# 32 bytes more per tile: operand and weight tiles of a float32 split-product kernel at other places in SBUF

## The chip, the cores and the metric

The kernel runs on one core of a Trainium2 chip. The metric is device time in microseconds (us). Two timed runs of the kernel before gave 1836.11 and 1837.32 us, a median of 1836.71 us. Durations of single instructions come from one further execution that the hardware profiler recorded.

## The reference

Two transformer-like blocks on 512 tokens of width 1024, all in float32. Nearly all of the work is matrix products of the activations with weight matrices; what lies between them is elementwise.

```
hn = rms_norm(h, g_mix_pre);  proj = hn @ w_in                 # 1024 -> 8192
br_a = spatial_gating(gelu(z_sgu)) @ w_sgu_out
br_b = conformer_conv(z_conv)      @ w_conv_out                # depthwise, 31 taps
br_c = multiscale_pool(z_pool)     @ w_pool_out
h = h + rms_norm((gates . (br_a, br_b, br_c)) @ w_out)
h = h + rms_norm((silu(f_gate) * f_up) @ w_ffn_out)            # 1024 -> 2 x 2816 -> 1024
h = h + sigmoid(h @ w_ple_gate) * (p @ w_ple)
# second block
proj = rmsnorm(x) @ w_in_2
oa = gated_delta_rule(conv(q, k, v))                           # a scan over chunks of 64 tokens, 4 heads
ob = chunk_band_attention(q, k, v)                             # 8 heads
x = x + (sig(ga) * (oa @ w_branch_a) + sig(gb) * (ob @ w_branch_b)) @ w_out_2
x = x + (silu(gate) * up) @ w_down                             # 1024 -> 2 x 2816 -> 1024
out = rmsnorm(x)
```

## The kernel before, in words

Activations lie feature-major in SBUF: a product with 1024 input features reads eight tiles of 128 partitions x 512 tokens. To keep float32 accuracy with the one-pass `float32r` matmul, each operand is split in a high and a low half, and each 128x128 piece of a product is three matmuls (`mm3`, lines 153 to 156): high weights by high operand (L154), high weights by low operand (L155), low weights by high operand (L156). The stationary side is a 128-column slice of a weight tile, the moving side is an operand tile of 512 tokens, or of 256 where `linear_halves` does the tokens in two halves. `linear_tm` (L325 to L327) has the sides changed: the operand is stationary and the weights move.

The tiles in question:

- `raw`: a weight chunk as it lands by DMA, 128 x 1024 float32, two buffers (`prep`).
- `whi`, `wlo`: its high and low half, four buffers each. ScalarE writes `whi` (L99), VectorE writes `wlo` as `raw - whi` (L102).
- `xh`, `xl` and `th`, `tl`: two sets of operand tiles, high and low half, eight buffers of 128 x 512 each (`pair`). Operands beyond eight tiles (the products over 2816 features) and a few others are `fh`, `fl`, which come from other pools by the same helper `blk`.

All of them come from pools that hand out buffers of a tag in turn. `emit` runs the steps in order and prepares weight chunks two steps ahead of the step that uses them, so that TensorE goes from one product to the next.

Where the tiles start, as the built program places them, in bytes within 256, buffer by buffer:

| tile | before | after the change |
|---|---|---|
| `whi` (4 buffers) | 32, 32, 32, 32 | 32, 64, 96, 128 |
| `wlo` (4 buffers) | 32, 32, 32, 32 | 160, 192, 224, 0 |
| `xh`, `th` (8 buffers each) | 32 in all | 0, 32, 64, 96, 128, 160, 192, 224 |
| `xl`, `tl` (8 buffers each) | 32 in all | 32 in all |
| `fh`, `fl` | 224 in all | 224 in all |
| `raw` | 32 in both | 32 in both |
| `w16` (small weights of L782, L783; eight slices of 64 bytes) | 224, 32, 96, 160, and again | the same |

A slice of 128 columns is 512 bytes and half a tile of tokens 1024, so that a slice starts at the same place within 256 bytes as its tile. The low-half tiles `xl`, `tl` keep their size; they lie behind eight longer tiles, that is 256 bytes further on.

Of the kernel before, what the change touches and what calls it, by code (L numbers as in the profile page):

```python
# [9 lines left out]
F32R = mybir.dt.float32r  # L10
# [5 lines left out]
P = 128  # L16
T = 512
D = 1024
# [24 lines left out]
def build(tc, d, out):  # L43
# [7 lines left out]
    wp = root.enter_context(tc.tile_pool(name="wp", bufs=1))  # L51
# [4 lines left out]
    S = {}  # L56
    ALL = slice(0, T)
    HALVES = (slice(0, T // 2), slice(T // 2, T))

    # ------------------------------------------------------------------ constants  # L60
    vec = const.tile([P, NVEC], F32, name="vec")
    gin = const.tile([P, NB], F32, name="gin")
    ident = const.tile([P, P], F32, name="ident")
# [3 lines left out]
        o, _ = VEC[name]  # L67
        return vec[:, o + i:o + i + 1]

    # ------------------------------------------------------------------ helpers  # L70
    def blk(pool, tag, bufs, dt=F32, shape=(P, T)):
        return pool.tile(list(shape), dt, tag=tag, bufs=bufs, name=tag)

    def tmp():
# [60 lines left out]
    def prep(src, hold=None):  # L135
        n = src.shape[-1]
        raw = wp.tile([P, D], F32, tag="raw", bufs=2, name="raw")
        nc.sync.dma_start(raw[:, :n], src)
        if hold is not None:
            hi, lo = [], []  # L140
            for c0 in range(0, n, T):
                h, l = hold(), hold()
                m = min(n - c0, T)
                split(raw[:, c0:c0 + m], h[:, :m], l[:, :m])
                hi.append(h)
                lo.append(l)
            return Parts(hi), Parts(lo)
        hi = wp.tile([P, D], F32R, tag="whi", bufs=4, name="whi")
        lo = wp.tile([P, D], F32R, tag="wlo", bufs=4, name="wlo")
        split(raw[:, :n], hi[:, :n], lo[:, :n])  # L150
        return hi, lo

# [30 lines left out]
        return out  # L183

    def rstd_tm(sqs, scale, c=ALL, out=None, tag=""):
        """1 / sqrt(scale * column sums + eps), tokens on partitions."""
        b0, b1 = c.start // P, c.stop // P
        ps = auxps()
        for b in range(b0, b1):
            for i, s in enumerate(sqs):  # L190
                pe.matmul(ps[:, b - b0:b - b0 + 1], s[:, (b - b0) * P:(b - b0 + 1) * P], ones[:, 0:1],
                          start=(i == 0), stop=(i == len(sqs) - 1))
        m = small.tile([P, b1 - b0], F32, tag="rs_m" + tag, bufs=2, name="rs_m")
        ts(m, ps[:, :b1 - b0], scale, EPS, ALU.mult, ALU.add)
        return rsqrt_small(m, [P, b1 - b0], out, tag)

    def rowcast(y):
        """the values of tokens on partitions, as rows on every partition."""
        nb = y.shape[1]
        r = auxps()  # L200
        for b in range(nb):
            pe.matmul(r[:, b * P:(b + 1) * P], y[:, b:b + 1].to_broadcast([P, P]), ident, start=True, stop=True)  # L202
        return r[:, :nb * P]
# [18 lines left out]
        def parts(self, c=ALL):  # L222
            return [self.acc[:, c]] + self.last

    # ------------------------------------------------------------------ step queue
    steps = []
    bgq = deque()

# [30 lines left out]
        return [(k0, min(kb, k0 + kmax)) for k0 in range(0, kb, kmax)]  # L259

    def linear(name, nbs, kb, xs, consume, bg=2400, tag="mm"):
        """n-blocks of a feature-major product: consume(n, psum, tokens)."""
        for n in nbs:
            st = {}
            for k0, k1 in kchunks(kb):
                def fn(wh, wl, n=n, k0=k0, k1=k1, st=st):
                    if k0 == 0:
                        st["ps"] = auxps(tag)
                    for k in range(k0, k1):
                        xh, xl = xs(k)  # L270
                        w = slice((k - k0) * P, (k - k0 + 1) * P)
                        mm3(st["ps"], wh[:, w], wl[:, w], xh, xl, k == 0, k == kb - 1)
                    if k1 == kb:
                        consume(n, st["ps"], ALL)

                step(fn, d[name][n][:, k0 * P:k1 * P], bg)

    def linear_halves(name, nbs, kb, xs, consume, then=None, hold=None):
        """like linear, the first half of the tokens for all of nbs, then the second."""
        held = {}  # L280
        for hf, c in enumerate(HALVES):
            order = [(n, k) for n in nbs for k in kchunks(kb)]
            if hf:
                order.sort(key=lambda nk: nk[1])
            for n, (k0, k1) in order:
                def body(n=n, k0=k0, k1=k1, c=c):
                    if k0 == 0:
                        held[n, "ps"] = mmps()
                    ps = held[n, "ps"][:, :T // 2]
                    wh, wl = held[n, k0]  # L290
                    for k in range(k0, k1):
                        xh, xl = xs(k)
                        w = slice((k - k0) * P, (k - k0 + 1) * P)
                        mm3(ps, wh[:, w], wl[:, w], xh[:, c], xl[:, c], k == 0, k == kb - 1)
                    if k1 == kb:
                        consume(n, ps, c)

                if hf == 0:
                    def fn(wh, wl, n=n, k0=k0, body=body):
                        held[n, k0] = (wh, wl)  # L300
                        body()

                    step(fn, d[name][n][:, k0 * P:k1 * P], hold=hold and hold(n, k0))
                else:
                    step(body)
            if then is not None:
                step(lambda c=c: then(c))

    def linear_tm(name, halves, kb, xs, consume, tag2, between=None):
        """token-major product: 512 output features at a time; consume(half, tb, psum)."""  # L310
        for hf in halves:
            st = {}
            cuts = [0, 1] if between is not None and hf == 0 else [0]
# [30 lines left out]
        nc.sync.dma_start(t, src)  # L344
        return t

    # ================================================================== first block: mixing
    hp = ExitStack()
    st1 = ExitStack()
    st2 = ExitStack()  # L350
# [55 lines left out]
        S["cv"] = [None] * NB  # L406
        S["v"] = [[None, None] for _ in range(NT)]

    # spatial gating
    def sgu_v(hf, tb, ps):  # L410
        t = blk(S["p1"], "vm", 8)
        act.activation(out=t, in_=ps, func=AF.Gelu_apprx_tanh, scale=S["Rtm"][:, tb:tb + 1])
# [21 lines left out]

    step(sgu_ln)

    # gated depthwise convolution
    def conv_gate(n, ps, c):
        S["csig"] = sgt()
        act.activation(out=S["csig"], in_=ps, func=AF.Sigmoid)  # L440
# [52 lines left out]
        split(t, hi, lo)  # L493
        S["B"][h] = (hi, lo)

    # gates and branches
    def gate(n, ps, c):
        S["sig"] = sgt()
        act.activation(out=S["sig"], in_=ps, func=AF.Sigmoid)
# [118 lines left out]
    w_out_post = post("g_mix_post", lambda: blk(S["pf"], "fh", 14))  # L618

    def to_ffn(c):  # L620
        """h += rms_norm(y) * g; the operand of the next product is h * g, its row factor S['R']."""
        r = rowcast(rstd_tm(S["ss"].parts(c), 1.0 / D, c))
        if c.start == 0:
            S["B"] = [pair("B") for _ in range(NB)]
            S["R"] = blk(small, "R", 1)
            S["ss2"] = SqSum(lambda c: blk(S["pf"], "sx", 2, shape=(P, T // 2)))
            S["ss2"].acc = blk(small, "sq", 3)
        for n in range(NB):
            y, h = S["y"][n][:, c], S["h"][n][:, c]
            tt(y, y, r, ALU.mult)  # L630
            tt(h, h, y, ALU.add)
            hi, lo = S["B"][n]
            split_scaled(h, v("g_ffn_pre", n), hi[:, c], lo[:, c])
        for n in range(NB):
            h = S["h"][n][:, c]
            if n == 0:
                act.activation(out=S["ss2"].acc[:, c], in_=h, func=AF.Square)
            else:
                S["ss2"].add(h, c)
        acopy(S["R"][:, c], rowcast(rstd_tm(S["ss2"].parts(c), 1.0 / D, c)))  # L640
        if c.start:
            S["f"] = [None] * NF
            S["sigs"] = {}
# [21 lines left out]
    for g in range(2):  # L665
        step(lambda wh, wl, g=g: ple(wh, wl, g), d["w_ple"][g])

    # ================================================================== first block: feed forward
    def f_pair(j, set_):
        if j >= 8:  # L670
            return blk(S["pf"], "fh", 14, F32R), blk(S["pf"], "fl", 14, F32R)
# [23 lines left out]
    linear("w_ffn_in", order[2:], 8, xb, f_in)  # L695
    ffn_post = post("g_ffn_post", lambda: blk(acts, "th", 8))

    # per-layer embedding
    S["xd"] = [None] * NB

    def to_ple(c):
# [41 lines left out]
    linear_halves("w_ple_gate", range(3), 8, xa, ple_gate)  # L743
    linear("w_ple_gate", range(3, NB), 8, xa, ple_gate)

    # ================================================================== second block: mixing
    st3 = ExitStack()

    def to_second():
# [122 lines left out]
        return gt, col, flip  # L872

    def sq_norm(hd, x, scale, by=None):
        """by / sqrt(scale * sum of squares along each block * by^2 + eps)."""
        ss = small.tile([P, NT], F32, tag=f"ss{hd % 2}", bufs=1, name="ss")
        sq = blk(S["p2"], f"Gdec{hd % 2}", 1)
        for b in range(NT):
# [7 lines left out]
        y = rsqrt_small(ss, [P, NT], tag=str(hd % 2))  # L886
# [1 line left out]
        return y  # L888

    def gdn_first(hd):  # L890
        """decays, A of (I + A), and what needs the queries, keys and values as they are.

        With k = s k' for a normalized key k, the rows of A take s^2, v takes s and the solution is s u;
        products of k' and s u are those of k and u.  The scale of a query is applied to its output."""
        G, gm = S["gd"], S["gm"]
        q, k, vf = S["g"][hd], S["g"][4 + hd], S["g"][8 + hd]
        B = HB
# [10 lines left out]
        s = sq_norm(hd, km, 1.0)  # L908
# [37 lines left out]
        G[hd] = (dec, dect, gl, kds, km, vm, bgk, qs)  # L946

    def gdn_second(hd):
        """(I + A)^-1 by doubling of its blocks, and the scan."""
        G, gm = S["gd"], S["gm"]  # L950
        q, k = S["g"][hd], S["g"][4 + hd]
        B = HB
# [192 lines left out]
    for n in range(NB):  # L1145
        step(lambda wh, wl, n=n: branches(wh, wl, n), d["w_branch"][n])

    # ================================================================== second block: feed forward
    hp2 = ExitStack()
    st4 = ExitStack()  # L1150

# [194 lines left out]
```

## Time and profile before

| | |
|---|---|
| median of the runs | 1836.71 us |
| span of the profiled execution, first to last instruction | 1834.6 us |
| TensorE busy | 1820.0 us, 99% of the span, 8932 matmuls |
| weight loads busy | 1507.2 us, 82% |
| VectorE busy | 1182.3 us, 64% |
| ScalarE busy | 750.4 us, 41% |
| granted TensorE clock, mean | 0.998 |

The profiled execution's own time is its span; what a timed run has around it is the 2.1 us between span and median. A matmul's row has the time at which it starts and a modelled duration; rows of successive matmuls overlap, since the duration holds the way through the array. What a matmul costs in a dense stretch is therefore the time from its start to the start of the next, called the step below, and not the duration in its row. A timeline row has the start in us, the duration in us, the engine, the line, the operation, the tiles (written <- read) and the shape. A windows row has the stretch, its length, and for each engine the busy time and the number of instructions that overlap the stretch.

### The profile page before, as it was taken

The page shows a single profiled execution, that of the slowest core. Times are in us where ns is not written, and L with a number is a line of the kernel's source. Part 1 is how long each engine was busy: PE and PEld are TensorE (multiplying, and loading weights), DVE is VectorE, ACT ScalarE, POOL GpSimd, SP SyncE. Part 2 cuts the span into 40 slices and gives each one's busy share as a digit, 9 for nine tenths or more (in the row PEclk, how much of TensorE's full clock was granted, in tenths as well). Part 3 has the DMA queues.
Part 4 walks back from the last instruction along what each step waited for, and adds up shares of the span by engine and source line. Part 5 has one row for each costly group of instructions (what it writes and reads, how often), then busy time and mean ns, then how long its engine had stood idle before and what let it go on. Part 6 is the DMA issues. An engine that isn't in the chain of part 4 may idle for free.

```text
span 1834.6 us, 22934 instructions
## 1 busy us (share of the span) xinstructions
PE 1820.0 (99%) x8932; PEld 1507.2 (82%) x8932; DVE 1182.3 (64%) x2050; ACT 750.4 (41%) x1233; POOL 0.7 (0%) x5
## 2 busy tenths in 40 slices
PE   9999999999999999999999999999999999999997
PEld 7888888888888888888897887777888888888887
DVE  6999967986548444442286784678636577777333
ACT  5442234326346232222254742686315444444221
POOL 0000000000000000000000000000000000000000
PEclk9999999999999999999999999999999999999999
DMA  5232222322343222223334112202245322222332
GB/s 194 101 113 94 93 82 102 109 99 79 107 171 115 102 93 95 101 87 95 106 136 174 58 64 87 74 30 77 97 153 191 123 99 95 94 101 91 94 95 67
DMA packets 62893, 189.73 MB, mean 103 GB/s; under 512 B 7232, under 2 KB 10432, under 8 KB 62784
## 3 DMA queue, kind: packets, MB, share of 16 engines
q1 hardware_dynamic: 56736, 177.53, 28.4%
q10 hardware_dynamic: 6048, 10.73, 1.8%
q8 instruction: 70, 1.15, 0.3%
q14 instruction: 39, 0.32, 0.1%
HBM read 176.70 MB, written 11.53 MB: 103 GB/s over the span
## 4 chain that ended last, share of the span: by engine, by line
PE 96%; DVE 2%; DMA 1%; ACT 1%; issue 0%; SPq 0%; DVEq 0%; ACTq 0%
PE mm L155 27%; PE mm L154 27%; PE mm L156 27%; PE att L1047 1%; PE att L1071 1%; PE g L967 1%; PE g L962 1%; PE att L156 1%; PE att L155 1%; PE att L154 1%; PE mm L326 1%; PE mm L327 1%; PE att L1065 1%; PE mm L325 1%; DMA raw<-in_w_sv 1%; PE aux L202 1%
## 5 line engine op out<-in xcount | busy, mean ns | idle before, releaser
L99 ACT ACTIVATE whi<-raw 128x1024 fp32r<-128x1024 f32 (+3 forms) x304 | 312.3, 1027 | 663.6 <-PE mm L155 401.0
L102 DVE TENSOR_TENSOR wlo<-raw,whi 128x1024 fp32r<-128x1024 f32 (+3 forms) x304 | 358.9, 1181 | 196.8 <-ACT whi L99 191.5
L154 PE MATMUL mm<-xh,whi 128*128 128x512 f32 (+1 forms) x1032 | 393.8, 382 | 0.0
L155 PE MATMUL mm<-xl,whi 128*128 128x512 f32 (+1 forms) x1032 | 393.2, 381 | 0.0
L156 PE MATMUL mm<-xh,wlo 128*128 128x512 f32 (+1 forms) x1032 | 393.1, 381 | 0.0
L154 PE MATMUL mm<-th,whi 128*128 128x512 f32 (+1 forms) x976 | 379.2, 389 | 0.0
L155 PE MATMUL mm<-tl,whi 128*128 128x512 f32 (+1 forms) x976 | 378.9, 388 | 0.1
L156 PE MATMUL mm<-th,wlo 128*128 128x512 f32 (+1 forms) x976 | 378.6, 388 | 0.0
L156 PEld LDWEIGHTS mm<-xh,wlo 128*128 128x128 f32 x1032 | 194.0, 188 | 37.5
L154 PEld LDWEIGHTS mm<-xh,whi 128*128 128x128 f32 x1032 | 193.9, 188 | 37.3 <-issue 0.2
L155 PEld LDWEIGHTS mm<-xl,whi 128*128 128x128 f32 x1032 | 194.0, 188 | 36.8 <-issue 0.2
L155 PEld LDWEIGHTS mm<-tl,whi 128*128 128x128 f32 x976 | 183.6, 188 | 36.6 <-issue 1.6
L156 PEld LDWEIGHTS mm<-th,wlo 128*128 128x128 f32 x976 | 183.6, 188 | 36.2 <-issue 2.0
L154 PEld LDWEIGHTS mm<-th,whi 128*128 128x128 f32 x976 | 183.5, 188 | 36.2 <-issue 2.0
L111 DVE SCALAR_TENSOR_TENSOR cv<-hc,vec,cv 128x507 f32<-128x507 f32 (+18 forms) x240 | 172.1, 731 | 4.2 <-ACT cv L448 0.6
L156 PE MATMUL mm<-fh,wlo 128*128 128x512 f32 (+1 forms) x252 | 91.5, 363 | 0.0
L154 PE MATMUL mm<-fh,whi 128*128 128x512 f32 (+1 forms) x252 | 91.3, 362 | 0.0
L102 DVE TENSOR_TENSOR sg<-mm,R 128x512 f32<-128x512 f32 (+1 forms) x43 | 29.0, 677 | 89.8 <-PE mm L156 89.8
L155 PE MATMUL mm<-fl,whi 128*128 128x512 f32 (+1 forms) x236 | 85.0, 360 | 0.0
L102 DVE TENSOR_TENSOR t<-mm,R 128x512 f32<-128x512 f32 x56 | 38.5, 687 | 53.0 <-PE mm L156 51.1
L102 DVE TENSOR_TENSOR t<-mm,sg 128x512 f32<-128x512 f32 (+1 forms) x31 | 20.8, 672 | 62.6 <-PE mm L156 62.5
L154 PEld LDWEIGHTS mm<-fh,whi 128*128 128x128 f32 x252 | 47.2, 187 | 8.3
(375 smaller groups left out, 2075.6 us busy)
## 6 DMA issues: line engine op xcount, KB each, us to landing
raw<-in_w_ffn_in SPq DMA_DIRECT2D x44, 512.0 KB, 3.2
raw<-in_w_up SPq DMA_DIRECT2D x44, 512.0 KB, 3.2
raw<-in_w_g SPq DMA_DIRECT2D x24, 512.0 KB, 3.2
raw<-in_w_out SPq DMA_DIRECT2D x16, 512.0 KB, 3.2
raw<-in_w_ffn_out SPq DMA_DIRECT2D x16, 512.0 KB, 3.5
raw<-in_w_gab SPq DMA_DIRECT2D x16, 512.0 KB, 3.3
raw<-in_w_down SPq DMA_DIRECT2D x16, 512.0 KB, 3.5
raw<-in_w_qkv SPq DMA_DIRECT2D x12, 512.0 KB, 3.2
```

The lines of the kernel that those rows point to most:

```text
L99: act.activation(out=o, in_=i, func=AF.Copy, scale=scale)
L102: dve.tensor_tensor(out=o, in0=a, in1=b, op=op)
L111: dve.scalar_tensor_tensor(out=o, in0=a, scalar=s, in1=b, op0=op0, op1=op1)
L154: pe.matmul(ps, wh, xh, start=first, stop=False)
L155: pe.matmul(ps, wh, xl, start=False, stop=False)
L156: pe.matmul(ps, wl, xh, start=False, stop=last)
L202: pe.matmul(r[:, b * P:(b + 1) * P], y[:, b:b + 1].to_broadcast([P, P]), ident, start=True, stop=True)
L325: pe.matmul(ps, xh[:, t], wh[:, c], start=(k == 0), stop=False)
L326: pe.matmul(ps, xh[:, t], wl[:, c], start=False, stop=False)
L327: pe.matmul(ps, xl[:, t], wh[:, c], start=False, stop=(k == kb - 1))
L962: pe.matmul(yp[:, B[b]], A[:, B[b]], Z[:, B[b]], start=True, stop=True)
L967: pe.matmul(zp[:, B[b]], Zt[:, B[b]], Y[:, B[b]], start=True, stop=True)
```

## The change

`blk` asks for tiles of 520 instead of 512 columns when the tag is `xh` or `th`, and hands out the first 512. `prep` does the same for `whi` and `wlo`, 1032 instead of 1024 columns. Eight float32 are 32 bytes, so that each further buffer of these tags starts 32 bytes later within 256 than the one before it (table above). All tiles that are allocated behind them move by a multiple of 256 bytes, and keep their place within 256. Comments and docstrings are left out in the changed file, and line numbers move by two. The instructions of each engine, their shapes and their order are the same in both programs.

```diff
     def blk(pool, tag, bufs, dt=F32, shape=(P, T)):
+        if tag in ("xh", "th"):
+            return pool.tile([P, T + 8], dt, tag=tag, bufs=bufs, name=tag)[:, :T]
         return pool.tile(list(shape), dt, tag=tag, bufs=bufs, name=tag)
...
-        hi = wp.tile([P, D], F32R, tag="whi", bufs=4, name="whi")
-        lo = wp.tile([P, D], F32R, tag="wlo", bufs=4, name="wlo")
+        hi = wp.tile([P, D + 8], F32R, tag="whi", bufs=4, name="whi")[:, :D]
+        lo = wp.tile([P, D + 8], F32R, tag="wlo", bufs=4, name="wlo")[:, :D]
         split(raw[:, :n], hi[:, :n], lo[:, :n])
```

## The prediction

> **What bounds the kernel now.** First the page: busy times, the granted clock, and the chain of work that ended last.
>
> ```profile
> span 1834.6 us, 22934 instructions
> PE 1820.0 (99%) x8932; PEld 1507.2 (82%) x8932; DVE 1182.3 (64%) x2050; ACT 750.4 (41%) x1233; POOL 0.7 (0%) x5
> PEclk9999999999999999999999999999999999999999
> PE 96%; DVE 2%; DMA 1%; ACT 1%; issue 0%; SPq 0%; DVEq 0%; ACTq 0%
> ```
>
> The chain is TensorE for 96% of the span, at full clock. So only what changes the step from one matmul to the next can move the time much. Then windows of dense stretches (columns as told above: PE, weight loads, DVE, ACT, POOL, then clock, DMA share, GB/s):
>
> ```profile
> 200.00:240.00 40.00, 40.00 (x178) 33.14 (x177) 38.90 (x52) 9.71 (x11) 0.00 (x0) 1.00 0.27 92
> 600.00:760.00 160.00, 160.00 (x708) 132.48 (x707) 75.06 (x90) 46.81 (x60) 0.00 (x0) 1.00 0.28 96
> 1500.00:1660.00 160.00, 160.00 (x708) 132.53 (x707) 116.83 (x148) 71.25 (x87) 0.00 (x0) 1.00 0.28 97
> ```
>
> Two of the 708 began before the window, so the step is 160/706 = 0.2266 us, and 40/176 = 0.227 us in the first. VectorE is busy 47%, 73% and 97% of these windows, and the step is the same: the other engines' traffic doesn't set it. What does? The groups by shape give the counts, and timeline rows the step beside other tiles.
>
> ```profile
> L154 PE MATMUL mm<-xh,whi 128*128 128x512 f32 x952 | 371.7, 390 | 0.0
> L154 PE MATMUL mm<-th,whi 128*128 128x512 f32 x928 | 365.7, 394 | 0.0
> L154 PE MATMUL mm<-fh,whi 128*128 128x512 f32 x184 | 72.5, 394 | 0.0
> L155 PE MATMUL mm<-fl,whi 128*128 128x512 f32 x168 | 66.2, 394 | 0.0
> L154 PE MATMUL mm<-xh,whi 128*128 128x256 f32 x80 | 22.1, 282 | 0.0
> L154 PE MATMUL mm<-th,whi 128*128 128x256 f32 x48 | 13.6, 286 | 0.0
> L154 PE MATMUL mm<-fh,whi 128*128 128x256 f32 x68 | 18.8, 277 | 0.0
> ```
>
> ```profile
> 847.52 0.39 PE L154 MATMUL mm<-fh,whi 128*128 128x512 f32 x1
> ...
> 857.32 0.39 PE L154 MATMUL mm<-xh,whi 128*128 128x512 f32 x1
> ...
> 903.81 0.28 PE L154 MATMUL mm<-xh,whi 128*128 128x256 f32 x1
> ...
> 904.89 0.28 PE L154 MATMUL mm<-xh,whi 128*128 128x256 f32 x1
> 906.33 0.28 PE L154 MATMUL mm<-fh,whi 128*128 128x256 f32 x1
> ...
> 907.91 0.28 PE L156 MATMUL mm<-fh,wlo 128*128 128x256 f32 x1
> ```
>
> The stretch of `fh`, `fl` from 847.52 to 857.32 is 14 k-blocks of three, 42 matmuls: 9.80/42 = 0.2333 us a step, against 0.2267 with `xh` or `th`, of the same shape, with the same weight buffers. With 256 columns it is the other way round: nine steps of `xh` in 1.08 us are 0.120, fourteen of `fh` in 1.58 us are 0.113. The one difference that I find between these operands is the place: `xh` starts at 32 within 256 bytes, as the weights do, `fh` at 224. So the step depends on where the operand lies against the weights, by 6.7 ns either way. All four settled steps are near multiples of that (34, 35, 18 and 17 times 6.67 ns). From 256 to 512 columns the step grows by 0.2267 - 0.120 = 106.7 ns at the least; streaming alone thus takes at most 2 x 106.7 = 213.3 ns, and at least 13.3 ns of each 226.7 is something else.
>
> I take it to be the two reads that run at once: the load of the next weights starts with the matmul, as these rows show, and both walk through SBUF.
>
> ```profile
> 700.27 0.39 PE L155 MATMUL mm<-tl,whi 128*128 128x512 f32 x1
> 700.27 0.19 PEld L156 LDWEIGHTS mm<-th,wlo 128*128 128x128 f32 x1
> ```
>
> By the Trainium skill, "TensorE: Matmul & The Clock Gate", section "Wait — 56ns, not 53.3ns?", a warm stream should step at N/2.4 GHz plus about 2.5 ns, measured 215.7 ns at 512 columns. The 226.6 above disagrees; what holds these matmuls back isn't on that page.
>
> **The change part by part.** It adds no instruction and moves none. It changes places alone.
>
> *Matmuls.* Before, the relation of operand to weights is one and the same for thousands of matmuls in a row, and the step settles at 226.7. After, it goes through the eight multiples of 32 bytes: from one k-block to the next `xh` moves on by 32, within a block L154 and L155 change between `xh` and `xl`, and L156 goes to another weight tile. Two places in the trace show matmuls that haven't settled.
>
> ```profile
> 127.34 0.39 PE L155 MATMUL mm<-xl,whi 128*128 128x512 f32 x1
> ...
> 129.18 0.39 PE L154 MATMUL mm<-xh,whi 128*128 128x512 f32 x1
> ...
> 131.00 0.39 PE L156 MATMUL mm<-xh,wlo 128*128 128x512 f32 x1
> 1005.70 0.40 PE L782 MATMUL g<-th,w 128*16 128x512 f32 x1
> ...
> 1009.41 0.40 PE L154 MATMUL mm<-th,whi 128*128 128x512 f32 x1
> ```
>
> Behind a break (the small matmuls up to 127.03) the next eight steps take 1.84 us, 230 ns each, and the eight after them 1.82 us, 227 ns. In L782 and L783 the stationary slices lie at 224, 32, 96 and 160 in turn, and 16 steps take 3.71 us: 231.9 ns each. That is the nearest row to what the change makes everywhere, though with 16 columns of weights. The bounds for a 512-column step after the change are 213.3 (streaming alone) below and 240 above (one 6.67 more than any settled step; no settled row is there, so this end is an estimate). I take 230: the middle of the two settled values, and what the unsettled steps behind a break show. I stay under 231.9 because a third of the new starts (half of `xh`, `th`) fall on multiples of 64, which no 512-column operand has now; the trace cannot price that.
>
> How many are settled now? L154 with `xh`, `th` counts 952 + 928, and L155 and L156 as many: 5640. In the scan and attention part matmuls come in short runs that break off:
>
> ```profile
> 1020.00:1120.00 100.00, 34.91 (x85) 16.01 (x85) 1.00 0.19 63
> 1150.00:1320.00 170.00, 43.15 (x104) 19.70 (x104) 1.00 0.20 69
> ```
>
> These are windows of L154 alone: 189, with L155 and L156 567 matmuls, unsettled already and left as they are. 5640 - 567 = 5073 at +3.3 ns: +16.9 us. Those with 256 columns, 3 x (80 + 48) = 384, go from 120 to 116.7, the middle of theirs: -1.3 us. `fh`, `fl` stay at 224, but the weights under them move: 184 x 2 + 168 = 536 from 233.3 to 230, -1.8 us; 204 with 256 columns from 113.3 to 116.7, +0.7 us.
>
> *The other engines.* They write and read the same tiles at the new places.
>
> ```profile
> L102 DVE TENSOR_TENSOR wlo<-raw,whi 128x1024 fp32r<-128x1024 f32 x278 | 339.6, 1222 | 143.2 <-ACT whi L99 137.9 <-DMA h<-in_xT 3.3
> L102 DVE TENSOR_TENSOR fl<-t,fh 128x512 fp32r<-128x512 f32 x28 | 19.3, 688 | 9.8 <-ACT fh L99 9.8
> L102 DVE TENSOR_TENSOR xl<-t,xh 128x512 fp32r<-128x512 f32 x23 | 15.3, 684 | 0.0
> L99 ACT ACTIVATE whi<-raw 128x1024 fp32r<-128x1024 f32 x278 | 294.8, 1060 | 591.6 <-PE mm L155 337.9 <-issue 170.7 <-PE att L155 14.7
> L99 ACT ACTIVATE fh<-t 128x512 fp32r<-128x512 f32 x30 | 18.7, 623 | 44.4 <-DVE t L102 38.5 <-issue 4.0 <-DMA t<-in_pT 1.8
> L99 ACT ACTIVATE xh<-t 128x512 fp32r<-128x512 f32 x23 | 14.1, 627 | 5.7 <-DVE t L102 4.6 <-DVE t L111 1.1
> ```
>
> A split to tiles at 224 takes 688 and 623 ns, to tiles at 32 684 and 627: no price on the place here, and I put it at nothing, between -1% and +1% of 339.6 + 294.8 us, 6 us either way. It is covered: a weight chunk's split is 2.28 us, the 24 matmuls that use a chunk take 5.44. Without that cover the whole 6 us would show.
>
> Sum: 16.9 - 1.3 - 1.8 + 0.7 = +14.5 us on the span of 1834.6, 1849.1. The median of the runs is 2.1 us above the span: **1851 us**, 0.8% slower.
>
> **The rivals.** Measurement tells 2%, 36.7 us, from no change; that is 7.2 ns on each of the 5073 matmuls.
>
> *Nothing changes.* The step has a cause that moves with neither tile, and `fh` differs for another reason, such as its pool or its products. Against it: 42 matmuls at 233.3 stand between stretches at 226.7 in one product, w_ffn_out. 1837 us. The Trainium skill says so too: "SBUF — State Buffer", section "Who interferes with whom", gives TensorE two independent read ports and states "PE and ACT never wait on anyone". The 847.52 rows speak against applying that here.
>
> *The spread takes meetings away.* If both reads starting at the same place is the bad case, and most other relations are better, a step falls by 6.7 ns to 220: 5073 x 6.7 = -34 us, 1803; by the full 13.3 it is -67 us, 1769. For it: 256 columns are faster with the operand elsewhere (113 against 120), and a multiple of 64 may read one piece less. Against it: at 512 columns, where most of the time is, elsewhere is slower. If only the third on multiples of 64 falls by one step, 5073/3 x 6.7 = -11 us, and 1826. The rate on the skill's TensorE page, 215.7 ns, would be the end of this road.
>
> *The spread adds meetings.* Slower, in the dense products w_in, w_ffn_in, w_up_2: where the relation never repeats, half of the matmuls pay 233.3 and half 240, a mean of 236.7: 5073 x 10 = +51 us, 1887. It decides from a mean of 233.9 on. For it: single unsettled steps are longer than any settled one, and L782/L783 stand at 231.9. Against it: no dense stretch of the trace has a mean of 236.
>
> **How the numbers follow.** Forecast 0.45, nothing 0.20, fewer meetings 0.20, more meetings 0.15. Fewer meetings brings over 2% in about half of its cases (a step below 219.5): 0.12 with a little from the cover being better than thought. More meetings is over 2% in nearly all, and the forecast's upper end, all at 233.3 (+34 us, 1871) with 6 us lost on the splits, adds a little: 0.17. That leaves 0.71 within 2%. The forecast's own range is 1840 (mean 227.3) to 1871. The range for 8 in 10 reaches down past one step less for all (1803, and 6 us for the splits) to 1797 and up past 233.3 for all to 1876; it leaves out about 0.05 below and 0.14 above.
>
> **What would show it.** With the forecast, the window from 600 to 760 us has some 698 matmuls in place of 708, steps no longer settle at one value, and `fh` and `xh` come closer together. 708 again means that nothing changed; 729 or more that 6.7 ns were saved on each; 686 or fewer that meetings were added. Steps on a multiple of 64 that differ from the others by 6.7 ns would price what I couldn't. I am wrong in the mechanism if the step follows the operand's place alone whatever the weights', and wrong in the size if unsettled steps behind a break were long for the break's sake and not for their phase.

## The result: 1.35% slower, and the profile after

The changed kernel took 1862.20 us (median of two runs, 1860.73 and 1863.68) against 1836.71 us: a ratio of 1.0135, 95% interval 1.0118 to 1.0151. The forecast was 1851 with a range of 1797 to 1876. The loss is clear of the noise, though under the 2% from which a change is called faster or slower here. The direction was right, and so was the place where the time goes, the matmul's step; the loss was 25.5 us where 14.3 were forecast. One run of the kernel before, among those beside e4 and e5 below, took 2258.29 us at a granted clock of 0.752 and is left out of all figures.

The page of the changed kernel, in the lines that answer to those of before. Line numbers are two higher: high weights by high operand is L156, high by low L157, low by high L158.

```profile
span 1859.0 us, 22934 instructions
PE 1845.6 (99%) x8932; PEld 1508.1 (81%) x8932; DVE 1183.5 (64%) x2050; ACT 748.8 (40%) x1233; POOL 0.7 (0%) x5
PE 97%; DVE 1%; DMA 0%; ACT 0%; issue 0%; SPq 0%; DVEq 0%; ACTq 0%
```

The span grew by 1859.0 - 1834.6 = 24.4 us, TensorE's busy time by 25.6. The other engines do the same work in the same time as before. So the matmuls themselves take longer, and the dense windows show by how much:

```profile
600.00:760.00 160.00, 160.00 (x693) 129.77 (x692) 73.43 (x91) 46.82 (x61) 0.00 (x0) 1.00 0.30 96
1500.00:1660.00 160.00, 160.00 (x693) 129.80 (x692) 114.93 (x145) 69.42 (x86) 0.00 (x0) 1.00 0.29 94
```

693 matmuls in place of 708. With the same two taken off, the step is 160/691 = 231.5 ns, 4.9 more than before, at the same full clock. The forecast's 5073 matmuls times 4.9 ns are 24.9 us, about the whole growth of the span. It doesn't matter that VectorE is busy 46% in one window and 72% in the other.

The timeline has stretches that no longer settle. Behind the break at 128 us, 20 steps of `xh` and `xl`, and later the stretch of `fh` and `fl` in w_ffn_out, first with 512 columns and then with 256:

```profile
128.17 0.39 PE L157 MATMUL mm<-xl,whi 128*128 128x512 f32 x1
...
132.82 0.40 PE L156 MATMUL mm<-xh,whi 128*128 128x512 f32 x1
...
846.47 0.39 PE L156 MATMUL mm<-fh,whi 128*128 128x512 f32 x1
...
856.23 0.39 PE L156 MATMUL mm<-xh,whi 128*128 128x512 f32 x1
...
920.43 0.28 PE L156 MATMUL mm<-fh,whi 128*128 128x256 f32 x1
...
925.36 0.28 PE L156 MATMUL mm<-xh,tl 128*128 128x256 f32 x1
```

The first 20 steps take 4.65 us, 232.5 ns each; before, the step was down to 227 after eight. The 42 steps of `fh`, `fl` take 9.76 us, 232.4 each (233.3 before), and the 42 with 256 columns 4.93 us, 117.4 each (such steps had a mean of 113.7 before).

The splits, by the groups of the page, are where they were. The tiles `whi`, `wlo` and `xh` now begin at up to eight places:

```profile
L104 DVE TENSOR_TENSOR wlo<-raw,whi 128x1024 fp32r<-128x1024 f32 x278 | 339.8, 1223 | 149.1 <-ACT whi L101 147.0
L104 DVE TENSOR_TENSOR xl<-t,xh 128x512 fp32r<-128x512 f32 x23 | 15.3, 685 | 0.0
L101 ACT ACTIVATE whi<-raw 128x1024 fp32r<-128x1024 f32 x278 | 294.9, 1061 | 610.4 <-PE mm L157 352.7 <-issue 175.8 <-PE att L157 15.2
L101 ACT ACTIVATE xh<-t 128x512 fp32r<-128x512 f32 x23 | 14.1, 629 | 5.7 <-DVE t L104 4.6 <-DVE t L113 1.1
```

1223, 685, 1061 and 629 ns, against 1222, 684, 1060 and 627. To VectorE and ScalarE these places make 2 ns at most.

### The profile page after: what moved, and what is told of

Its sections match the earlier page's. It is cut to its first block, busy times and chain, and to the rows that moved or that the text cites. A ratio compares the mean times of both kernels' runs of the same rounds, so it can differ in the third digit from the quotient of the medians.

```text
span 1859.0 us, 22934 instructions
## 1 busy us (share of the span) xinstructions
PE 1845.6 (99%) x8932; PEld 1508.1 (81%) x8932; DVE 1183.5 (64%) x2050; ACT 748.8 (40%) x1233; POOL 0.7 (0%) x5
## 4 chain that ended last, share of the span: by engine, by line
PE 97%; DVE 1%; DMA 0%; ACT 0%; issue 0%; SPq 0%; DVEq 0%; ACTq 0%
PE mm L158 28%; PE mm L157 28%; PE mm L156 28%; PE att L1049 1%; PE att L1073 1%; PE g L969 1%; PE g L964 1%; PE att L158 1%; PE att L156 1%; PE att L157 1%; PE mm L328 1%; PE mm L329 1%; PE att L1067 1%; PE mm L327 1%; PE aux L204 0%; DMA raw<-in_w_sv 0%
## 5 line engine op out<-in xcount | busy, mean ns | idle before, releaser
L156 PE MATMUL mm<-xh,whi 128*128 128x512 f32 (+1 forms) x1032 | 397.6, 386 | 0.0
L157 PE MATMUL mm<-xl,whi 128*128 128x512 f32 (+1 forms) x1032 | 397.4, 385 | 0.0
L158 PE MATMUL mm<-xh,wlo 128*128 128x512 f32 (+1 forms) x1032 | 397.4, 385 | 0.0
L157 PE MATMUL mm<-tl,whi 128*128 128x512 f32 (+1 forms) x976 | 382.2, 392 | 0.0
L156 PE MATMUL mm<-th,whi 128*128 128x512 f32 (+1 forms) x976 | 382.1, 392 | 0.0
L158 PE MATMUL mm<-th,wlo 128*128 128x512 f32 (+1 forms) x976 | 382.0, 391 | 0.0
L157 PEld LDWEIGHTS mm<-xl,whi 128*128 128x128 f32 x1032 | 193.8, 188 | 41.7 <-issue 0.2
L156 PEld LDWEIGHTS mm<-xh,whi 128*128 128x128 f32 x1032 | 193.6, 188 | 41.8 <-issue 0.2
L158 PEld LDWEIGHTS mm<-xh,wlo 128*128 128x128 f32 x1032 | 193.8, 188 | 41.3
L157 PEld LDWEIGHTS mm<-tl,whi 128*128 128x128 f32 x976 | 183.5, 188 | 40.1 <-issue 1.6
L156 PEld LDWEIGHTS mm<-th,whi 128*128 128x128 f32 x976 | 183.5, 188 | 39.7 <-issue 2.0
L158 PEld LDWEIGHTS mm<-th,wlo 128*128 128x128 f32 x976 | 183.6, 188 | 39.4 <-issue 2.0
L158 PE MATMUL mm<-fh,wlo 128*128 128x512 f32 (+1 forms) x252 | 92.0, 365 | 0.0
L156 PE MATMUL mm<-fh,whi 128*128 128x512 f32 (+1 forms) x252 | 91.7, 364 | 0.0
L157 PE MATMUL mm<-fl,whi 128*128 128x512 f32 (+1 forms) x236 | 85.2, 361 | 0.0
L158 PEld LDWEIGHTS mm<-fh,wlo 128*128 128x128 f32 x252 | 47.4, 188 | 8.2
```

The source lines that it names most:

```text
L156: pe.matmul(ps, wh, xh, start=first, stop=False)
L157: pe.matmul(ps, wh, xl, start=False, stop=False)
L158: pe.matmul(ps, wl, xh, start=False, stop=last)
```

## The experiments

Two kinds of kernel were run. Five are the whole kernel with tiles at other places and the same instructions. Three others (m1, m2, m3) have groups of 49 matmuls added behind w_up_2, each group at one choice of places, sizes or types; nobody reads what these compute, and they lengthen the kernel, so that only their own steps count and not the time of the run. "Relation" below is the start of the operand (the moving side) less the start of the weights (the stationary side), within 256 bytes: 0 for `xh` and `th` before the change, 192 for `fh` and `fl`.

### Each half of the change alone

e1: the operands' tiles alone are longer.

```diff
     def blk(pool, tag, bufs, dt=F32, shape=(P, T)):
+        if tag in ("xh", "th"):
+            return pool.tile([P, T + 8], dt, tag=tag, bufs=bufs, name=tag)[:, :T]
```

> The longer tiles for xh and th alone; the weight tiles as before, all at 32. Theory (a step settles only where the relation of operand to weights repeats): within a k-block L154 and L156 stand at one relation and L155 at another, and the first changes from block to block, so nothing settles: 230 to 232 ns a step, 1853 to 1862 us. Rival (it is the weights' changing places that cost): 226.7 as before, 1837 us. Rival (the moving operand's own place costs): the whole of the change's 1862 us.

e2: the weight buffers alone.

```diff
-        hi = wp.tile([P, D], F32R, tag="whi", bufs=4, name="whi")
-        lo = wp.tile([P, D], F32R, tag="wlo", bufs=4, name="wlo")
+        hi = wp.tile([P, D + 8], F32R, tag="whi", bufs=4, name="whi")[:, :D]
+        lo = wp.tile([P, D + 8], F32R, tag="wlo", bufs=4, name="wlo")[:, :D]
```

> The longer weight tiles alone; all operands at 32 as before. Theory (settling needs a repeating relation): the relation changes twice in a k-block (L154 and L155 one weight tile, L156 the other), with a period of three matmuls, so steps are mixed, 228 to 233 ns, 1845 to 1865 us. Rival (the operand's own place alone sets the step): 226.7, 1837 us.

Measured: e1 1862.68 us, ratio 1.0140 (1.0123 to 1.0157); e2 1863.56, 1.0145 (1.0130 to 1.0160). The window from 600 to 760 us, of e1:

```profile
600.00:760.00 160.00, 160.00 (x694) 129.74 (x693) 74.18 (x91) 46.11 (x60) 0.00 (x0) 1.00 0.28 98
```

and of e2:

```profile
600.00:760.00 160.00, 160.00 (x692) 129.94 (x691) 73.56 (x91) 45.91 (x61) 0.00 (x0) 1.00 0.28 97
```

Each half by itself costs as much as both: 160/692 = 231.2 and 160/690 = 231.9 ns a step. So the cost is neither in the operands' place nor in the weights', and the two don't add: it is enough that one side moves against the other. e1 lies just above its range of 1853 to 1862 us, and its time alone would also fit the rival there, that the operand's own place costs; e2, in which the operands stay where they were, rules that rival out.

### Both sides moved together

e3: 32 bytes more in front of all these tiles. `xh`, `xl`, `th`, `tl`, `whi` and `wlo` start at 64 in place of 32, `fh` and `fl` at 0 in place of 224. Every absolute place is another; every relation is as before.

```diff
+    const.tile([P, 8], F32, name="pad")
```

> One idle tile of 32 bytes ahead of all these tiles: weights and operands all start at 64 instead of 32 within 256 bytes, fh and fl at 0 instead of 224; every relation is as before. Theory (the relation decides): steps 226.7 and 233.3 as before, 1837 us. Rival (a start on a multiple of 64 saves one piece of reading): 220 ns a step, some 1800 us.

Measured: 1836.84 us, ratio 0.9999 (0.9989 to 1.0008). Its window:

```profile
600.00:760.00 160.00, 160.00 (x707) 132.48 (x707) 74.91 (x90) 46.57 (x60) 0.00 (x0) 1.00 0.28 96
```

707 matmuls, against 708 before the change. What counts is where the operand starts relative to the weights; moving all by the same 32 bytes costs nothing.

### Another relation, always the same

The reason given in the prediction was that a step settles because its relation repeats. e5 takes that apart: nothing is spread, every `xh`, `xl`, `th`, `tl` starts at 160 and all weights at 32, relation 128 throughout (and 64 for `fh`, `fl`).

```diff
+    acts.tile([P, 32], F32, name="pad")
```

> An idle tile of 128 bytes ahead of the operand tiles: all of xh, xl, th, tl at 160, weights at 32, one relation of 128 for every matmul, fh and fl at 96 (relation 64). Nothing is spread, every relation repeats. Theory now (relation 0 is the one good place, and any other costs about what the spread costs): 233.4 on 5073 matmuls, +34 us, less 2 us on fh and fl and some tenths on 256 columns: 1867 to 1869 us. Rival (what costs is that the relation changes from matmul to matmul, a repeated one settles): 1837 us or a little less.

Measured: 1866.30 us, just under the range given; ratio 1.0158 (1.0142 to 1.0174), no cheaper than the spread itself (1.0135, 1.0118 to 1.0151). Its windows:

```profile
600.00:760.00 160.00, 160.00 (x695) 129.77 (x694) 75.52 (x103) 47.05 (x61) 0.00 (x0) 1.00 0.29 99
1500.00:1660.00 160.00, 160.00 (x690) 129.74 (x689) 115.26 (x146) 70.23 (x88) 0.00 (x0) 1.00 0.27 96
```

160/693 = 230.9 ns and 160/688 = 232.6. One short stretch, first and last matmul:

```profile
651.66 0.40 PE L156 MATMUL mm<-tl,whi 128*128 128x512 f32 x1
...
653.29 0.40 PE L157 MATMUL mm<-th,wlo 128*128 128x512 f32 x1
```

Here seven steps take 1.63 us; by the starts in the trace they are 240, 233, 231, 231, 229, 230 and 232 ns, and the next seven run through much the same values. So a relation that repeats need not settle at one step, and its mean is as dear as that of relations that change. Repetition alone doesn't buy the 226.7. Whether relation 0 alone does is asked of m2 below.

### The price of each relation

m1: 49 matmuls for each relation, and some with both sides moved, with other sizes, and with one side that changes its place from one matmul to the next. `xh` is the stationary side here and `wh` moves; the first columns of each set the places.

```diff
+        for _ in range(49): pe.matmul(ps[:128, :512], xh[:, 0:128], wh[:, 0:512], start=True, stop=True)
+        for _ in range(49): pe.matmul(ps[:128, :512], xh[:, 0:128], wh[:, 8:520], start=True, stop=True)
...
+        for _ in range(49): pe.matmul(ps[:128, :512], xh[:, 8:136], wh[:, 8:520], start=True, stop=True)
...
+        for _ in range(49): pe.matmul(ps[:16, :512], xh[:, 0:16], wh[:, 0:512], start=True, stop=True)
...
+        for i in range(49): pe.matmul(ps, xh[:, i % 8 * 8:i % 8 * 8 + P], wh[:, 0:T], start=True, stop=True)
```

> The kernel before with 32 added lines of 49 matmuls each behind the product w_up_2, whose results nobody reads: the same shapes at chosen places, 8 relations in steps of 32 bytes, three with both sides moved, 4, 8 and 16 bytes, 64, 32 and 16 weight columns, 256 and 384 moving columns, and four lines in which one side changes place from matmul to matmul. The time grows by some 0.36 ms for the added work. Theory (two reads meet by their relation): the step settles at a multiple of 6.67 ns that depends on the relation alone, 226.7 at 0, 233.3 at 192, the same when both sides move; it falls to 213 to 220 with 16 weight columns; lines in which one side changes place don't settle and have 230 to 233. Rival (the moving side's place alone): steps follow the moving side's start and not the weights', and not the weights' number of columns.

The timeline of m1, where equal instructions in a row are drawn together: start of the first, time to the end of the last, and the count.

```profile
1699.23 11.27 PE L1211 MATMUL mm<-whi,xh 128*128 128x512 f32 x49
1710.34 11.60 PE L1212 MATMUL mm<-whi,xh 128*128 128x512 f32 x49
1721.77 11.39 PE L1213 MATMUL mm<-whi,xh 128*128 128x512 f32 x49
1733.00 11.59 PE L1214 MATMUL mm<-whi,xh 128*128 128x512 f32 x49
...
1790.19 11.32 PE L1219 MATMUL mm<-whi,xh 128*128 128x512 f32 x49
...
1914.74 11.52 PE L1230 MATMUL mm<-whi,xh 128*16 128x512 f32 x49
...
1937.49 11.51 PE L1232 MATMUL mm<-whi,xh 128*16 128x512 f32 x49
...
1988.84 11.59 PE L1239 MATMUL mm<-whi,xh 128*128 128x512 f32 x49
2000.27 11.61 PE L1240 MATMUL mm<-whi,xh 128*128 128x512 f32 x49
2011.71 11.51 PE L1241 MATMUL mm<-whi,xh 128*128 128x512 f32 x49
2023.06 11.43 PE L1242 MATMUL mm<-whi,xh 128*128 128x512 f32 x49
```

From start to start L1211 (relation 0) takes 11.11 us for 49 steps, 226.7 ns; L1212 (32) 11.43, 233.3. The mean of the last 16 steps of each group, when they repeat, in ns:

| relation, bytes | 0 | 32 | 64 | 96 | 128 | 160 | 192 | 224 |
|---|---|---|---|---|---|---|---|---|
| 512 columns | 226.7 | 233.3 | 229.0 | 233.2 | 233.3 | 234.3 | 233.3 | 233.4 |
| 256 columns | 120.0 | | 117.8 | | 118.4 | | 113.4 | |

"Repeat" is not "settle": by the single starts, only relations 0 and 192 stay within 1 ns of one value at 512 columns. At 64 the steps run 226, 229, 232 in turn, at 96 they run 232, 237, 231, and at 128 they change between 229 and 238. So these prices are means over a cycle, and 229.0 or 234.3 are no multiples of 6.67: that part of the theory fell. With both sides moved by 32, 64 or 224 (L1219 to L1221) the step settles at 226.7 again, as e3 said for the whole kernel; the first eight steps of these groups have means of 230 to 231.

Relation 0 is the best of the eight at 512 columns, and the mean of the eight is (226.7 + 233.3 + 229.0 + 233.2 + 233.3 + 234.3 + 233.3 + 233.4)/8 = 232.1. By the table of places, the change deals out relations 0, 160, 192 and 224 twice as often as the other four; so weighted the mean is 232.0, and the change measured 231.5. That they come close doesn't show that each matmul pays its own relation's price: in the changed kernel's own trace the dense matmuls at relation 0 step at 231.0, and the eight relations lie between 229.4 and 233.2.

With one side walking over eight places and the other fixed, the last 16 steps of L1239 and L1240 are 233.3 and 234.2, above the 230 to 233 that were expected; with two places in turn, 32 bytes apart (L1241) or 128 (L1242), they are 231.6 and 230.0. With 16 weight columns the step was expected to fall to 213 to 220. It rose to 231.7, the same at both relations that were tried: (11.52 - 0.39)/48 = 231.9 at relation 0 (L1230), (11.51 - 0.39)/48 = 231.7 at 192 (L1232), and 231.7 and 231.6 over the last 16.

m2 asks whether it is a matmul's relation to its own weights or to the next one's, since those are loaded while it runs. Both sides walk over the eight places, with relation 0 to its own weights, to the next matmul's weights, or to neither; last, the change's own order of places in threes.

```diff
+        for i in range(49): pe.matmul(ps, xh[:, i % 8 * 8:i % 8 * 8 + P], wh[:, i % 8 * 8:i % 8 * 8 + T], start=True, stop=True)
+        for i in range(49): pe.matmul(ps, xh[:, (i - 1) % 8 * 8:(i - 1) % 8 * 8 + P], wh[:, i % 8 * 8:i % 8 * 8 + T], start=True, stop=True)
+        for i in range(49): pe.matmul(ps, xh[:, (i + 1) % 8 * 8:(i + 1) % 8 * 8 + P], wh[:, i % 8 * 8:i % 8 * 8 + T], start=True, stop=True)
...
+        for i in range(48):
+            k, j = i // 3, i % 3
+            pe.matmul(ps, xh[:, (8 if j == 2 else 40):][:, :P], wh[:, (0 if j == 1 else k % 8 * 8):][:, :T], start=True, stop=True)
```

> The kernel before with added lines of 49 matmuls whose results nobody reads, as in the first such run: both sides changing place together from matmul to matmul, with the relation to the own weights kept at 0, then the relation to the next weights at 0, then neither; two PSUM banks in turn; 16, 96, 112 and 120 weight columns; 128 to 448 moving columns; relations of 3, 12, 20, 63, 60 and 62 elements and of 256 and 320 bytes; the weights' second half; and the change's own order of three matmuls at its places. Theory (the load that runs beside a matmul meets its reads, and that is the next matmul's load): the line with the next weights at relation 0 has 226.7, the line with the own weights doesn't. Rival (own weights): the other way round. Rival (the places must repeat, the relation alone is not enough): 230 to 234 in both. Two PSUM banks change nothing unless writing back is what costs. Relation 256 is as 0 and 320 as 64. The change's order gives 231 to 232.

The timeline of m2; L1211 to L1213 are the three walks, L1214 is relation 0 at fixed places, with two PSUM banks in turn, and L1241 is the change's own order:

```profile
1702.09 11.63 PE L1211 MATMUL mm<-whi,xh 128*128 128x512 f32 x49
1713.56 11.48 PE L1212 MATMUL mm<-whi,xh 128*128 128x512 f32 x49
1724.88 11.47 PE L1213 MATMUL mm<-whi,xh 128*128 128x512 f32 x49
1736.19 11.30 PE L1214 MATMUL mm<-whi,xh 128*128 128x512 f32 x49
...
1978.40 11.28 PE L1241 MATMUL mm<-whi,xh 128*128 128x512 f32 x48
1989.52 11.31 PE L1244 MATMUL mm<-whi,xh 128*128 128x512 f32 x48
```

11.47, 11.32 and 11.31 us for 49 steps: 234.1, 231.0 and 230.8 ns. Relation 0 to a matmul's own weights doesn't help when the places move, and relation 0 to the next one's helps no more than neither. Neither reading of "own" or "next" holds: of the places in steps of 32 bytes, only relation 0 at places that stay came down to 226.7. L1214 does so too once it has settled (226.7 over the last 16), so two PSUM banks in turn change nothing. The change's own order of places (L1241) takes 1989.52 - 1978.40 = 11.12 us for 48 steps, 231.7 ns, close to the 231.5 of the changed kernel. No group in m1 or m2 with 512 columns of four bytes has a mean below 226.7.

### What the rest of a step is

m3 asks where the time beyond the columns themselves sits. Beside a control (L1212): two-byte elements at relations 0, 64 and 192 and with 16 weight columns (L1213 to L1216); four-byte elements with the moving side one column read 512 times (L1217); and with the weights one column read 128 times, relation 0 and 192 (L1218, L1219).

```diff
+        xb, wb = xh.bitcast(mybir.dt.bfloat16), wh.bitcast(mybir.dt.bfloat16)
+        for i in range(49): pe.matmul(ps, xb[:, 0:P], wb[:, 0:T], start=True, stop=True)
...
+        for i in range(49): pe.matmul(ps, xh[:, 0:P], wh[:, 0:1].to_broadcast([P, T]), start=True, stop=True)
+        for i in range(49): pe.matmul(ps, xh[:, 0:1].to_broadcast([P, P]), wh[:, 0:T], start=True, stop=True)
```

> The kernel before with eight added lines of 49 matmuls whose results nobody reads: the same tiles as before in relation 0 as a control; the same bytes read as bfloat16 at relations 0, 64 and 192 and with 16 weight columns; float32r with one moving column repeated 512 times; float32r with one weight column repeated 128 times, at relations 0 and 192. Theory (what is lost beside 213 ns is lost in reading four bytes per column of the moving side, and the place of the load only sets how the loss settles): control 226.7; bfloat16 214 to 217 at every place; one moving column repeated 213 to 220; repeated weight column 226 to 233 whatever the place. Rival (the loss is the meeting of the two reads): the repeated weight column takes it away, 213 to 220. Rival (the loss is the float32r pass itself): one moving column repeated has 227 to 233 as well.

Its timeline:

```profile
1700.67 11.27 PE L1212 MATMUL mm<-whi,xh 128*128 128x512 f32 x49
1712.01 10.52 PE L1213 MATMUL mm<-whi,xh 128*128 128x512 bf16 x48
1722.37 10.74 PE L1214 MATMUL mm<-whi,xh 128*128 128x512 bf16 x48
1732.94 10.74 PE L1215 MATMUL mm<-whi,xh 128*128 128x512 bf16 x48
1743.61 10.74 PE L1216 MATMUL mm<-whi,xh 128*16 128x512 bf16 x49
1754.28 10.98 PE L1217 MATMUL mm<-whi,xh 128*128 128x512 f32 x49
1765.10 11.39 PE L1218 MATMUL mm<-whi,xh 128*128 128x512 f32 x49
1776.33 11.49 PE L1219 MATMUL mm<-whi,xh 128*128 128x512 f32 x49
```

Each of the groups here with a count of 48 has 49 matmuls, of which one record is missing in the trace; L1213's row begins with its second. A group's time less its last matmul's own duration, over 48 steps: (10.74 - 0.38)/48 = 215.8 ns for two-byte elements, whatever the relation or the number of weight columns. The control is (11.27 - 0.39)/48 = 226.7, so 10.9 ns lie between the two; the 13.3 of the prediction counted from 213.3, which no group here reached. With one moving column repeated the step is 220.6, and 218.6 over the last 16: most of the 10.9 ns is gone with four-byte elements too. With one weight column repeated it is (11.39 - 0.39)/48 = 229.2 at relation 0 and (11.49 - 0.39)/48 = 231.3 at 192, where m1 has 226.7 and 233.3 with all columns: most of the loss stays.

Two-byte elements also make the weight load shorter (98 ns in its rows in place of 188), which would be another reason for their 215.8. But m1's loads of 16 four-byte columns take 95 ns, and their matmuls step at 231.7. So most of the time beyond 215.8 hangs on the moving side, on reading a new four-byte element for each column; making the weight load short or small doesn't take it away, though its place and its size still shift it.

### A better place for `fh` and `fl`

If relation 0 is best at 512 columns, the 536 matmuls of `fh`, `fl` at 192 lose 6.7 ns each. e4 moves these two by 64 bytes, to 32, and leaves the rest as before the change.

```diff
+    small.tile([P, 16], F32, name="pad")
```

> An idle tile of 64 bytes in the pool behind the operand tiles, so that fh and fl start at 32 within 256 bytes instead of 224, in relation 0 to the weights as xh and th are; all else keeps its relation. Theory (relation 0 is the good place at 512 columns and a bad one at 256): 536 matmuls of 512 columns from 233.3 to 226.7, -3.6 us, 204 of 256 columns from 113.3 to 120, +1.4 us, together -2.2 us, 1834.9 us. Rival (the pool's own place or the products' order made the 233.3): no change, 1837 us.

Measured: 1834.90 us, 1.9 us less than the kernel before beside it (1836.80), ratio 0.9990 (0.9981 to 0.9999). The stretch of `fh` and `fl` in w_ffn_out, first and last matmul:

```profile
846.88 0.39 PE L155 MATMUL mm<-fh,whi 128*128 128x512 f32 x1
...
856.18 0.39 PE L157 MATMUL mm<-fh,wlo 128*128 128x512 f32 x1
```

41 steps in 9.30 us, 226.8 ns each, where they had been 233.3. Adding up all starts, `fh` and `fl` with 512 columns gave 3.5 us and took 1.3 more with 256, as reckoned. This is the fastest version that was run, by a tenth of a per cent, which is far less than the 2% that decide here and close to its own sum of 2.2 us.

## Why the prediction was right, and where it was short

**The bound and the kind of effect: right.** TensorE's step sets the time, and the change moves nothing but that step. The whole growth is in the step: adding up all starts, the matmuls of `xh`, `xl`, `th`, `tl` with 512 columns took 24.4 us more, which is the growth of the span.

**The term that was mis-sized: 230 ns for an unsettled step.** It measured 231.5. So 5073 x 3.3 = 16.9 us should have been 5073 x 4.9 = 24.9. The measured 231.5 lies between the 230 taken and the 233.3 of the forecast's upper end. The 230 was the middle of two settled values, and what backed it were the first eight steps behind a break. Those are on their way down to 226.7, as the first eight of L1219 to L1221 in m1 are, so they don't show what places cost that never stop changing; the prediction had named this as the way in which its size could be wrong. The row that I had called the nearest, L782 and L783 at 231.9, would have given 5073 x 5.2 = 26.4 and a sum within 2 us of the result, but by luck: m1 has 231.7 for 16 weight columns at places that stay, so its 16 columns are enough for that row, whether places change or not. I went below it for the third of the starts on multiples of 64, for which I had no row. After the change the mean step of the dense matmuls (those with a step under 260 ns) of `xh` and `th` with 512 columns, by where the operand starts, in ns:

| operand starts at | 0 | 32 | 64 | 96 | 128 | 160 | 192 | 224 |
|---|---|---|---|---|---|---|---|---|
| step | 232.0 | 231.6 | 232.6 | 231.5 | 230.0 | 231.6 | 230.8 | 232.4 |

The four multiples of 64 have a mean of 231.4, the four others 231.8: there was next to nothing to take off. The window had 693 matmuls, five under the forecast's 698, which is the same error again.

**The small terms.** `fh` and `fl` with 512 columns came to 232.4, not 230: -0.5 us in place of -1.8. Their 204 with 256 columns went from 113.7 to 118.2: +0.9 us by the starts, +0.7 forecast. The 384 of `xh`, `xl`, `th`, `tl` with 256 columns went from 119.7 to 118.2: -0.5, forecast -1.3. `fh` and `xh` did come close together. The splits cost nothing, as taken. With these terms the sum is 24.4 - 0.5 + 0.9 - 0.5 = 24.3 us, against 24.4 measured on the span and 25.5 on the medians.

**The reason: half right.** That the step follows the relation of operand and weights is shown by e3 (nothing, though all places moved) and by e1 and e2 (either side alone costs the whole). That it is cheap because the relation repeats is refuted by e5: a relation of 128 that never changes cost 29.5 us. m2's first walk shows that places that stay are needed as well, since relation 0 at changing places steps at 234.1. Before the change both held, by the pools' sizes alone. So the sign of the forecast rested in part on luck: that the relation before was also the best of the eight, the prediction didn't know.

**"The two reads that run at once": not shown.** m3 and the 16-column groups speak against a meeting of two long reads: most of the loss stays when the weight load reads an eighth of the columns, in half the time, or one column again and again, and goes when the moving side does the latter (218.6). How the place and the size of the load act on the step stays open; no run here resolves it.

**The rivals.** "Nothing changes" is out: the interval begins at 1.0118. The Trainium skill's "PE and ACT never wait on anyone" ("SBUF — State Buffer", section "Who interferes with whom") doesn't cover this: no other engine came into it, and still a place was worth 6.6 ns a step. "Fewer meetings" is out: no relation that was run at 512 columns is better than 0. "More meetings" had the sign, but at 236.7 it was further off than the forecast, and at 231.5 it doesn't decide (it needed 233.9). The rate of 215.7 that the Trainium skill gives in "TensorE: Matmul & The Clock Gate", section "Wait — 56ns, not 53.3ns?", is what two-byte elements do here (215.8); four-byte elements never reached it.

## What to carry to other kernels

In a stream of `float32r` matmuls with 512 columns, keep operand and weights at the same place within 256 bytes, at every buffer: a pad that spreads buffers over places cost 1.4% here, and a pad that brought two stray tiles into line gained 0.1%. With 256 columns it is the other way round (last section). Before a row of the profile prices a new state, ask in what else it differs from that state: one row here, with 16 weight columns, had the right number for another reason, and another was still on its way to a settled value. Read such costs as steps from start to start: the modelled duration of a matmul stays at 0.39 or 0.40 us while its step moves from 226.7 to 234.

## What the runs showed that I had not expected

- A constant wrong relation is as dear as a changing one: 1866.3 us (e5) and 1862.2 (the change), against 1836.8 and 1836.7 of the kernel before beside each.
- Relations aren't symmetric: 64 has a mean of 229.0, 192 one of 233.3. With 256 columns the order turns about: 113.4 at 192 and 120.0 at 0, so that the 204 such matmuls of `fh`, `fl` were best off where they lay.
- Finer shifts count too. m1 and m2 have 236.7 at a relation of 4 bytes, 233.4 at 8 and 231.7 at 16, but 226.7 at -4 and at -16, and 230.0 at -8. So 0 isn't the only good relation, and no run here says why these are. At 256 bytes it is 226.7 as at 0, and at 320 it is 228.9, close to the 229.0 at 64, which is why I speak of places within 256.
- A load of 16 weight columns makes the step longer, not shorter: 231.7 against 226.7 with 128 columns, both at relation 0. The widths between don't lie on a line: 230.4 with 64, 230.0 with 96 and 233.2 with 120 columns.
